# Two tiles share each gate/up block, memory folding in per-head units, casts and x spills in small pieces

## Chip, cores, metric

The kernel runs on the 8 cores of one Trainium2 chip, the same program on each with its own half of a sequence. The metric is the device time of the slowest core in microseconds (us). Most executions agree within 0.3%. Some fall into a slower state, in which one die (cores 0 to 3 or 4 to 7) or both show a lower granted TensorE clock. Fast runs are compared with fast runs.

## The reference, cut

```python
for l in range(2):                                        # D=1024, D_FF=2816, float32 inputs
    x = x + 0.5 * swiglu(rms_norm(x), gate1[l], up1[l], down1[l])      # FFN 1
    h = rms_norm(x); q, k, v, u = split(h @ w_in[l])
    x = x + concat(norm(window_attention(q, k, v)), norm(pooling(u))) @ w_out[l]
    x = x + memory_cross_attention(rms_norm(x), rms_norm(mem), wq[l], wkv[l], wo[l])
    x = x + 0.5 * swiglu(rms_norm(x), gate2[l], up2[l], down2[l])      # FFN 2
return rms_norm(x)
```

## The kernel before

A core computes 4224 tokens in 9 tiles of 512 or 384. Its weights come as float32 blocks, 128 x 2048. A cast DMA on the GpSimd (POOL) queue makes bf16 of a block at first use; a block that is used again is written back as bf16 and from then on loaded from there on the SyncE (SP) queue. Blocks land in a ring of 6 buffers for the FFN (`sb_fr`) and of 4 for the rest (`sb_mr`).

The program is a list of "visits". Each has FFN 2 of tile t-1, the mixer of tile t and FFN 1 of tile t+1, interleaved, so that TensorE has FFN matmuls while the mixer's other engines work. I number them: visit 1 is FFN 1 of tile 0 alone, visit 2 has the mixer of tile 0 and FFN 1 of tile 1, visit 3 is the first with all three, and so on to 20. The second layer's mixer begins in visit 11.

All waits are made by one helper from records of what was last written and read; an engine executes its waits and its DMA issues in program order:

```python
def dma(self, qn, out_ap, in_ap, reads=(), writes=(), box=None):
    e = self.E[qn]
    self._wait(e, self._deps(reads, writes))     # for the last writer AND readers of all of `writes`
    ...
    e.h.dma_start(out=out_ap, in_=in_ap).then_inc(box.sem, 16)
```

Which blocks are cast, and which of them are written back (`s` is the number of the block, `occ` counts its earlier uses):

```python
KEEP = 17
def route(kind, a, s, occ):          # -> (cast from float32, write back as bf16)
    if kind == "wf" and a == 0:      # FFN 1 of the first layer
        if occ == 0: return True, s >= KEEP
        if occ == 1 and s < KEEP: return True, True
    elif kind == "wf" and a == 1 and occ == 0: return True, True
    ...
```

The second layer's weights are cast in the background, three blocks (1.5 MB) to a DMA; x is stored and loaded as one DMA of up to 2 MB per tile:

```python
def load_x(v):   ... P.dma("pool", xs[s][:, :, :T], src[:, :, c0:c0 + T], ...)
def store_x(ti, l): ... P.dma("pool", x1_d[:, :, c0:c0 + T], xs[s][:, :, :T], ...)
```

Memory folding makes, once per layer, the products of memory's keys and values with the query and output weights. It runs whole in the visit of tile 0's mixer. Its last part stores each output block in four pieces:

```python
for s in range(4):
    P.dma("pool", dv[:, s, :, h, :], sv[:, s, :, :], reads=(ob_,), writes=(wabuf[l][4 + h],), box=...)
```

The order inside a visit, around x and the rope tables (sines and cosines of the positions, for the rotation of q and k; `ropes[0]` loads the positions, the rest computes, mostly on VectorE):

```python
fs += merge(gu1[6:], final_steps(*F2) + [load_x(v + 2)] + segw + seg3 + ropes)   # cut
```

The softmax here doesn't subtract the row's maximum and nothing guards it: scores larger than these inputs give would overflow.

## Time and profile before

5436.08 us, median of 6 runs (5428.8 to 5441.26).

Three lines of the page's second part, in 40 slices of the 5429.4 us span: busy tenths of TensorE, its granted clock, and the busy share of the DMA engines.

```profile
PE   7766999999999989999999899999999999999988
PEclk9887999999999999999999999999999999999999
DMA  9973975857666776887755545444454545455545
```

TensorE is at its limit nearly everywhere except in the first four slices. The table of stretches of the same core, cut at visits 1, 2, 3, then 4 to 10, visit 11, and so on; busy time (and instructions) of each engine, granted clock, DMA share, GB/s:

```profile
core 3: us, PE busy (x) PEld busy (x) DVE busy (x) ACT busy (x) POOL busy (x), PEclk, DMA share, GB/s
0.00:167.00 167.00, 126.89 (x537) 52.85 (x537) 44.19 (x75) 32.65 (x51) 41.11 (x61) 0.98 0.96 190
167.00:544.20 377.20, 241.31 (x1110) 109.75 (x1110) 118.14 (x193) 111.48 (x181) 78.34 (x104) 0.81 0.69 158
544.20:863.10 318.90, 302.26 (x1419) 134.62 (x1418) 141.31 (x217) 89.60 (x147) 60.52 (x71) 0.99 0.80 208
863.10:2841.70 1978.60, 1915.93 (x9868) 946.18 (x9866) 887.70 (x1479) 579.05 (x1006) 308.92 (x322) 0.99 0.70 195
2841.70:3174.40 332.70, 305.29 (x1639) 157.54 (x1637) 130.96 (x212) 114.58 (x203) 63.94 (x69) 0.97 0.54 185
```

And what TensorE waited for, in all, in the list of waits (total us, times, longest):

```profile
PE ps L343 <- POOL sb_ach L448: 70.0, 32, 15.2
PE ps L343 <- DMA sb_mr<-wx: 39.9, 7, 14.2
PE ps L343 <- DMA sb_fr<-wfb: 39.4, 11, 9.5
PE ps L343 <- DMA sb_fr<-wf: 33.2, 24, 4.3
```

The reader should see that visit 2 (167 to 544 us) has a clock of 0.81 and 241 us of matmul in 377. `sb_mr<-wx` are the folding's casts, `sb_fr<-wfb` loads of ready bf16 weights, `sb_ach` the sum of squares in front of a norm.

A measure used from here on: the **loss** of a visit is its duration less the columns of its matmuls divided by 2.4 GHz. All matmuls together carry 4962 us of columns. A full visit of 512-tiles in the second layer took 304.3 us for 297.6 of columns, a loss of 6.7. Of this about 3.6 us is the rate: in the trace a group of eight 512-column matmuls follows the last after 1.727 us, 215.9 ns each, where 512/2.4 is 213.3, and 2.6/213.3 of 297.6 is 3.6. The Trainium skill, "TensorE: Matmul & The Clock Gate", Part 1, gives N / 2.4 GHz + about 2.5 ns for warm matmuls, and the trace agrees.

### The profile page before, as it was taken

Reading aid. Unit: us, or ns where it says so; the run is one execution under the profiler, and the core shown is the slowest. Engines: PE = TensorE matmul, PEld = TensorE weight load, DVE = VectorE, ACT = ScalarE, POOL = GpSimd, SP = SyncE. Lnnn points to the kernel's source line nnn. Section 1 sums busy time; section 2 is a strip of 40 time slices with the busy share of each in tenths; the row PEclk is TensorE's granted clock in tenths of the full one; section 3 lists DMA queues with packets and bytes.
Section 4 is the critical chain, followed back from the end, with each engine's and each line's share of the span. In section 5 each row is a group of like instructions: output and inputs, shape, how many; then the busy total and the mean of one; then the engine's idle time right before and its main releaser. Section 6 shows DMA issues by size and latency. Waiting matters only on the chain.

```text
span 5429.4 us, 79466 instructions; the slowest of 8 cores (5401.3 to 5429.4 us)
## 1 busy us (share of the span) xinstructions
PE 5073.9 (93%) x25858; PEld 2481.2 (46%) x25858; DVE 2335.9 (43%) x3804; ACT 1645.2 (30%) x2816; POOL 980.7 (18%) x1065
## 2 busy tenths in 40 slices
PE   7766999999999989999999899999999999999988
PEld 3232444444444444555545444444444445455545
DVE  2422534445453534453536144453535344445353
ACT  1232222223232222233323323232323223233342
POOL 2212212111111112011111121211111121212211
PEclk9887999999999999999999999999999999999999
DMA  9973975857666776887755545444454545455545
GB/s 184 216 167 104 227 217 155 207 168 194 168 191 189 186 206 179 233 217 226 216 167 200 176 165 171 149 169 152 136 182 144 175 150 187 163 197 190 197 156 166
DMA packets 258878, 983.42 MB, mean 181 GB/s; under 512 B 29648, under 2 KB 30048, under 8 KB 256768
## 3 DMA queue, kind: packets, MB, share of 16 engines
q1 hardware_dynamic: 216000, 784.00, 44.1%
q0 software_dynamic: 41904, 193.29, 17.6%
q8 instruction: 222, 3.64, 0.3%
q14 instruction: 176, 1.44, 0.1%
q10 hardware_dynamic: 576, 1.05, 0.1%
HBM read 996.44 MB, written 134.35 MB: 208 GB/s over the span
## 4 chain that ended last, share of the span: by engine, by line
PE 79%; DMA 12%; DVE 3%; ACT 3%; issue 2%; POOL 1%; DVEq 0%; ACTq 0%; POOLq 0%; SPq 0%
PE ps L343 79%; DMA sb_fr<-wfb 3%; DMA sb_fr<-wf 3%; DMA wfb<-sb_fr 2%; DMA wab<-sb_mr 2%; ACT sb_tmp L149 1%; POOL sb_ach L448 1%; DMA sb_mr<-wx 1%; ACT sb_sqf L149 1%; POOL sb_acc L448 0%; ACT L146 0%; DVE sb_pT L986 0%; DMA sb_x<-xT 0%; DMA sb_ao<-memT 0%; DMA sb_mr<-wm 0%
## 5 line engine op out<-in xcount | busy, mean ns | idle before, releaser
L343 PE MATMUL ps<-sb_hF,sb_fr 128*128 128x512 bf16 (+1 forms) x12672 | 2629.3, 364 | 68.2 <-DMA sb_fr<-wfb 36.9
L343 PEld LDWEIGHTS ps<-sb_hF,sb_fr 128*128 128x128 bf16 x12672 | 1243.9, 98 | 1353.6 <-issue 122.1
L343 PE MATMUL ps<-sb_act,sb_fr 128*128 128x512 bf16 (+1 forms) x6336 | 1322.9, 363 | 22.2 <-DMA sb_fr<-wf 17.3
L528 DVE TENSOR_TENSOR sb_act<-ps,sb_sg 128x512 bf16<-128x512 f32 (+1 forms) x792 | 508.0, 645 | 1379.9 <-PE ps L343 1092.5
L448 POOL TENSOR_TENSOR sb_acc<-sb_acc,sb_sqf 128x512 f32<-128x512 f32 (+2 forms) x528 | 633.1, 1201 | 2176.4 <-ACT sb_sqf L149 2172.5
L343 PEld LDWEIGHTS ps<-sb_act,sb_fr 128*128 128x128 bf16 x6336 | 615.6, 98 | 679.1 <-issue 63.4
L343 PE MATMUL ps<-sb_hM,sb_mr 128*128 128x512 bf16 (+1 forms) x3600 | 786.1, 364 | 48.0 <-DVE sb_hM L476 27.5
L149 ACT ACTIVATE sb_sg<-ps 128x512 f32<-128x512 f32 (+1 forms) x792 | 438.6, 558 | 1153.6 <-PE ps L343 988.1
L149 ACT ACTIVATE sb_sqf<-sb_x 128x512 f32<-128x512 f32 (+1 forms) x560 | 330.5, 592 | 1019.6 <-DVE sb_x L863 438.8
L343 PEld LDWEIGHTS ps<-sb_hM,sb_mr 128*128 128x128 bf16 x3600 | 353.8, 98 | 419.5 <-issue 66.0
L149 ACT ACTIVATE sb_pT<-ps 128x512 bf16<-128x512 f32 (+2 forms) x436 | 233.8, 567 | 359.0 <-PE ps L343 357.3
L564 DVE SCALAR_TENSOR_TENSOR sb_x<-ps,sb_x 128x512 f32<-128x512 f32 (+1 forms) x288 | 184.7, 642 | 283.6 <-PE ps L343 282.7
L343 PE MATMUL ps<-sb_pT,sb_mr 128*128 128x512 bf16 (+2 forms) x1280 | 259.3, 354 | 33.6 <-DVE sb_pT L986 23.1
L476 DVE SCALAR_TENSOR_TENSOR sb_hF<-sb_x,sb_vecs,sb_rst 128x512 bf16<-128x512 f32 (+1 forms) x288 | 227.3, 841 | 11.6 <-ACT sb_rst L149 11.6
L986 DVE TENSOR_TENSOR sb_pT<-sb_pT,sb_tmp 128x512 bf16<-128x512 bf16 (+1 forms) x144 | 101.2, 744 | 302.2 <-ACT sb_tmp L149 278.4
L343 PEld LDWEIGHTS ps<-sb_pT,sb_mr 128*128 128x128 bf16 x1280 | 124.7, 98 | 161.2 <-issue 47.9
L476 DVE SCALAR_TENSOR_TENSOR sb_hM<-sb_x,sb_vecs,sb_rst 128x512 bf16<-128x512 f32 (+1 forms) x288 | 185.6, 707 | 3.8 <-ACT sb_rst L149 3.8
L149 ACT ACTIVATE sb_tmp<-sb_tmp 128x512 f32<-128x512 f32 (+1 forms) x204 | 125.8, 617 | 161.2 <-DVE sb_tmp L783 147.8
L1014 DVE TENSOR_TENSOR sb_x<-ps,sb_x 128x512 f32<-128x512 f32 (+1 forms) x144 | 93.2, 647 | 184.2 <-PE ps L343 184.2
L448 POOL TENSOR_TENSOR sb_ach<-sb_acc,sb_sqf 128x512 bf16<-128x512 f32 (+2 forms) x100 | 116.6, 1166 | 303.6 <-PE ps L343 156.7
L863 DVE TENSOR_TENSOR sb_x<-ps,sb_x 128x512 f32<-128x512 f32 (+1 forms) x144 | 92.7, 644 | 138.1 <-PE ps L343 138.1
L652 DVE TENSOR_TENSOR sb_tmp<-ps,sb_sin 64x512 f32<-64x512 f32 (+1 forms) x180 | 116.0, 644 | 48.0 <-PE ps L343 36.2
(97 smaller groups left out, 2211.7 us busy)
## 6 DMA issues: line engine op xcount, KB each, us to landing
sb_fr<-wfb SPq DMA_DIRECT2D x1105, 512.0 KB, 4.3
sb_mr<-wmb SPq DMA_DIRECT2D x153, 512.0 KB, 4.4
sb_mr<-wab SPq DMA_DIRECT2D x144, 512.0 KB, 4.3
sb_fr<-wf POOLq DMA_DIRECT2D x83, 512.0 KB, 15.0
wfb<-sb_fr SPq DMA_DIRECT2D x66, 512.0 KB, 12.3
wfb<-wf POOLq DMA_DIRECT2D x22, 1536.0 KB, 17.4
x<-sb_x POOLq DMA_DIRECT2D x6, 2048.0 KB, 14.5
sb_x<-x POOLq DMA_DIRECT2D x6, 2048.0 KB, 11.2
```

Source lines behind the costliest of these rows:

```text
L149: return self.op("act", lambda h: h.activation(out=out, in_=in_, func=func, scale=scale, **kw), reads, writes)
L343: P.op("pe", lambda h: h.matmul(out_ap, lt, rh, start=st, stop=sp_, skip_group_check=True), reads=list(rb), writes=(ob_,), signal=(i == n ...
L448: P.op("pool", lambda h: h.tensor_tensor(out=o[:, :T], in0=acc[a][:, :T], in1=sqf[s][:, :T], op=ALU.add), (accb[a], sqfb[s]), (ob_,))
L476: P.op("dve", lambda h: h.scalar_tensor_tensor(out=out_ap, in0=in_ap, scalar=vcol(col), in1=r[0], op0=ALU.mult, op1=ALU.mult), (in_b, r[1] ...
L528: P.op("dve", lambda h: h.tensor_tensor(out=actF[:, hc, :T], in0=d[1][0][:, :T], in1=sg[si][:, :T], op=ALU.mult), (d[1][1], sgb[si]), (act ...
L564: P.op("dve", lambda h: h.scalar_tensor_tensor(out=x_, in0=pp[:, :T], scalar=0.5, in1=x_, op0=ALU.mult, op1=ALU.add), (ppb, xb_), (xb_,))
L652: P.op("dve", lambda h: h.tensor_tensor(out=t1[lo:lo + 64, :T], in0=pp[hi:hi + 64, :T], in1=sinS[pr][lo:lo + 64, :T], op=ALU.mult), (ppb, ...
L863: P.op("dve", lambda h: h.tensor_tensor(out=x_, in0=pp[:, :T], in1=x_, op=ALU.add), (ppb, xb_), (xb_,))
L986: P.op("dve", lambda h: h.tensor_tensor(out=pT[:, pi_, :T], in0=pT[:, pi_, :T], in1=tmp[i][:, :T], op=ALU.mult), (pTb[pi_], tmpb[i]), (pTb ...
L1014: P.op("dve", lambda h: h.tensor_tensor(out=x_, in0=pp[:, :T], in1=x_, op=ALU.add), (ppb, xb_), (xb_,))
```

## The change

Its intent: make the start cheaper and smooth the bursts.

1. The first two tiles (the second is now a 384 tile) both use a gate/up block when it arrives, in visit 1. Tile 1's activations are laid over the x buffer of tile 2.
2. The folding is divided into a preparation and four units, one per head. The first layer's go between the shared gate/up blocks of visit 1, the second layer's one each into visits 6 to 9.
3. Background casts are single blocks (512 KB), x moves in four pieces.
4. Rope tables have another order, and the norms' sum matmuls come half a down group later.

The diff, cut to its core:

```diff
+    sizes.insert(1, sizes.pop())                      # tile 1 is a 384 tile
-        def convert(kind, a, s0, s1):                  # three blocks
+        def convert(kind, a, s):                       # one block
         def load_x(v):
-            P.dma("pool", xs[s][:, :, :T], src[:, :, c0:c0 + T], reads=rd, writes=tuple(xbs[s]), box=xbox[s])
+            def piece(j):
+                cs = slice(j * CPP, (j + 1) * CPP)
+                ex = tuple(a2b) if v == 2 else ()      # tile 1's activations lie over this buffer
+                P.dma("pool", xs[s][:, cs, :T], src[:, cs, c0:c0 + T], reads=rd, writes=tuple(xbs[s][cs]) + ex, box=xbox[s][j])
+            return [(lambda j=j: piece(j), 0.1) for j in range(NPC)]
@@ visits
-                seg3 = memkv_steps(M[1]) if M[0] == 0 else []
+            seg3 = unit_at.get(v, [])
+            if v == -1:                                # visit 1
+                ...
+                for hc in range(3, HCH):
+                    fl += g0[3 * hc:3 * hc + 3] + g1[3 * hc:3 * hc + 3]
+                kv0 = memkv_prep(0)
+                for h in range(4):
+                    kv0 += memkv_unit(0, h)
+                run(sprinkle(merge(fl, kv0), ...))
+                run(raw(f_dn(0, 0, 1, ("mix", 0, 0))))
-                fs += merge(gu1[6:], final_steps(*F2) + [(lambda v=v: load_x(v + 2), 0.1)] + segw + seg3 + ropes)
+                fs += merge(gu1[6:], pre_at.get(v, []) + final_steps(*F2) + segw + load_x(v + 2) + ropes + seg3)
@@ tail_steps
-            out = raw(dn[:1]) + xs_[:1] + raw(dn[1:3]) + ...
+            out += raw(dn[:2]) + xs_[:1] + raw(dn[2:4]) + ...
     [cut: rope order, act_second, first_norm for two tiles, y in pairs, first-visit loads]
```

Not in the diff: KEEP stays 17.

## The prediction

> **What bounds the kernel now.** TensorE: 93% busy (the page's busy table), 79% of the chain that ended last. Its matmuls carry 4962 us of columns at 2.4 GHz, so of the 5429 us span 467 us are not columns. I cut the trace of the slowest core into 20 visits (gate/up and down of one tile beside the mixer of another) and subtracted each visit's columns:
> - first visit (first FFN of tile 0): 167 us for 115 of columns; 28 us pass before the first gate matmul, and the down part runs at 4.9 us per cast block against 3.45 of matmul;
> - second visit (FFN of tile 1, mixer of tile 0, memory folding): 377 for 211. The table of stretches gives TensorE 66%, 74%, 43% in 200-500 us at a granted clock of 0.78, 0.86, 0.69. The list of waits names the folding's casts (39.9), a late norm of memory (15.2), hM (24.8), the first mixer weight (17.6);
> - third visit: 22 lost, its FFN 2 cast at 4.8 us per block;
> - 1778-2842 us: 69 lost, 33 of it waits for FFN weights, 15 to 38 us in flight instead of 4.3 while a 2 MB x spill, a 2 MB x load and 1.5-2 MB casts overlap;
> - second layer's folding visit (2842-3174): 37, the chain goes through wab stores;
> - the rest is near its floor: 6.7 per visit, of which 216 instead of 213 ns per matmul is 3.6.
>
> **What the change does.**
> 1. Tiles 0 and 1 use the same gate/up blocks. The second visit loses tile 1's 22 gate/up casts and their 75 us of matmul; tile 1 becomes a 384 tile, so 56 us move to visit one. 17 casts with write-back move to visit three, which then casts 50 blocks.
> 2. First layer's folding (27 us of columns) becomes filler beside gate/up, at 7 us of matmul per block, so its casts have time.
> 3. Second layer's folding is spread over four steady visits.
> 4. Casts of 512 KB, x in four pieces: bursts fit the six-block ring.
> 5. Down halves go ahead of the stat matmuls, which wait 1.8 us twice per visit.
>
> **Estimates from those durations.** Visit one: 28 start + 8 waiting for tile 1's norm + 165 (131 gate/up, 27 folding, clock slightly reduced) + 45 down = 246. Visit two: tile 0's mixer with 28 us of filler, so a chain: projections and rope 38, attention 33, output projection 17, cross attention 45, norms 14, part of the filler: 155. The Trainium skill, "TensorE: Matmul & The Clock Gate", Part 1, says an idle window halves the clock; the trace agrees (0.69 in 400-500 us), so visit two stays slow. Together 401 against 544: -143. Visit three +8. Spill region -34. Second folding -27, +6 in the four visits. Stat waits -25. End -4. Sum -219: 5436 to about 5220 us (-4%), nearly all on the critical path, since TensorE's idle time is what goes.
>
> **Right or wrong in the profile.** Visit one near 246 us, TensorE over 85% from 50 us on; visit two near 155, clock under 0.9, no waits for folding casts; the spill region's loss under 40; no dip at 3000-3130 us; waits for the stat sum from 70 to under 35 us.
>
> **What would make it wrong.** Folding casts queueing behind FFN casts on one issuing queue; visit two's bare chain longer than 155; 50 casts in visit three exceeding the DMA (+20); small pieces contending as much as large ones.

## The result

5366.41 us, median of 10 runs (5362.21 to 5374.76), against 5430.53 us for the kernel before in the same rounds (20 runs). Ratio 0.9879, 95% interval 0.9871 to 0.9888. A ratio is the mean of one kernel's fast runs over the mean of the other's fast runs of the same rounds, so it isn't quite the ratio of the medians. It is faster by 1.2% (the interval excludes 1); I had forecast about 5220 us, 4% less.

The page's three lines after, of the 5373.2 us span:

```profile
PE   7678899999999999999999999999999999999998
PEclk9889999999999999999999999999999999999999
DMA  7768977666576666777655545554444445454655
```

The low stretch is shorter but has not gone. Stretches cut at the same visits (after visit 1 ends at 300.5, visit 2 at 448.1, visit 3 at 797.2, visits 4 to 10 at 2854.9, visit 11 at 3102.5):

```profile
core 1: us, PE busy (x) PEld busy (x) DVE busy (x) ACT busy (x) POOL busy (x), PEclk, DMA share, GB/s
0.00:300.50 300.50, 221.38 (x1122) 112.36 (x1123) 66.04 (x128) 70.97 (x132) 59.19 (x98) 0.93 0.79 154
300.50:448.10 147.60, 111.13 (x533) 51.06 (x530) 83.30 (x139) 51.53 (x87) 39.89 (x43) 0.91 0.61 164
448.10:797.20 349.10, 297.18 (x1399) 134.81 (x1400) 126.11 (x216) 79.16 (x139) 69.55 (x96) 0.94 0.88 215
797.20:2854.90 2057.70, 1992.90 (x10113) 970.21 (x10111) 911.62 (x1494) 621.01 (x1073) 394.19 (x459) 0.99 0.67 195
2854.90:3102.50 247.60, 242.42 (x1414) 134.75 (x1412) 117.68 (x203) 79.78 (x143) 45.66 (x47) 1.00 0.59 193
```

And the waits that answer to those shown of before:

```profile
PE ps L351 <- DMA sb_fr<-wf: 52.0, 24, 11.6
PE ps L351 <- DVE sb_act L566: 42.6, 9, 7.6
PE ps L351 <- POOL sb_ach L458: 35.0, 23, 5.1
PE ps L351 <- DMA sb_mr<-wx: 33.4, 6, 10.1
```

Further down the same list:

```profile
PE ps L351 <- DMA sb_fr<-wfb: 2.4, 1, 2.4
```

Much came as intended: waits for ready weights fell from 39.4 to 2.4, for the sum of squares from 70.0 to 35.0. But the folding's casts are still waited for, the FFN's casts more than before, and `sb_act` is new.

Loss by visit, the median of the six cores whose traces have every matmul:

| visits | before | after |
|---|---|---|
| 1 | 51.9 | 95.5 |
| 2 | 163.0 | 47.8 |
| 3 | 22.0 | 69.7 |
| 4 to 10 (sum) | 81.4 | 89.0 |
| 11 | 38.7 | 7.9 |
| 12 to the end (sum) | 97.8 | 85.0 |

Visits 2 and 11 gave 146 us together. Visits 1 and 3 took 91 back, and visits 4 to 10 gained nothing. Three places of the trace suggest why; the experiments test each.

**Visit 1.** The GpSimd queue in order of time (start, duration, count, idle before it and what ended that):

```profile
119.03 0.69 POOL L160 DMA_DIRECT2D wab<-sb_mr  x1 [2.01 <-ACT sb_sg L150]
128.10 0.70 POOL L160 DMA_DIRECT2D wab<-sb_mr  x1 [8.39 <-DMA wab<-sb_mr]
130.90 0.67 POOL L160 DMA_DIRECT2D wab<-sb_mr  x1 [2.10 <-DMA wab<-sb_mr]
133.56 0.67 POOL L160 DMA_DIRECT2D wab<-sb_mr  x1 [1.99 <-DMA wab<-sb_mr]
134.15 0.65 POOL L160 DMA_DIRECT2D sb_mr<-wx  x1
```

The four stores of a folded block wait for one another to land, because they name one record. The next cast of folding weights stands behind them: 15 us pass between the first store and that cast. In all the queue waited 51.7 us for such landings in visit 1.

**Visit 3.** The DMA share was 1.0 from about 480 to 720 us. It casts 50 blocks where it cast 33 before, as the 17 blocks below KEEP get their second cast here, and are written back here.

**Visits 4 to 9.** The same queue, then VectorE, in visit 4:

```profile
969.55 2.96 POOL L160 DMA_DIRECT2D sb_x<-xT  x4
972.50 0.57 POOL L160 DMA_DIRECT2D sb_tmp<-posr  x1
973.06 1.04 POOL L160 DMA_DIRECT2D wxb<-wx  x2
```

```profile
986.74 0.43 DVE L636 CAST sb_sin<-sb_tmp 128x512 f32<-128x512 int32 x1 [17.32 <-DMA sb_tmp<-posr]
```

The load of positions (256 KB) is now issued right behind the four pieces of x (2 MB). It lands 14 us later, and VectorE, whose next instruction needs it, does nothing for 17.3 us. Products of gate and up wait behind it, PSUM (the buffer that TensorE writes to) isn't freed, and TensorE waits for `sb_act`. In the kernel before, x was loaded earlier in the visit and the positions landed a median of 6.9 us after issue, against 13.7 now. VectorE waited for them there too, but 6.5 to 10.5 us at a time in visits 4 to 9 and not 17 to 18, and TensorE's waits for `sb_act` were 2.5 us in all.

### The profile page after: what moved, and what is told of

It is laid out like the page before. It is cut to its first block, busy times and chain, and to the rows that moved or that the text cites. A ratio compares the mean times of both kernels' runs of the same rounds, so it can differ in the third digit from the quotient of the medians.

```text
span 5373.2 us, 79736 instructions; the slowest of 8 cores (5336.6 to 5373.2 us)
## 1 busy us (share of the span) xinstructions
PE 5078.7 (95%) x25865; PEld 2485.2 (46%) x25865; DVE 2321.3 (43%) x3808; ACT 1620.3 (30%) x2800; POOL 1038.1 (19%) x1163
## 4 chain that ended last, share of the span: by engine, by line
PE 80%; DMA 10%; DVE 3%; issue 2%; ACT 2%; POOL 1%; DVEq 0%; ACTq 0%; POOLq 0%; SPq 0%
PE ps L351 80%; DMA sb_fr<-wf 3%; DMA sb_tmp<-posr 2%; DMA wab<-sb_mr 2%; DMA wfb<-sb_fr 2%; ACT sb_tmp L150 1%; DVE sb_hF L486 1%; POOL sb_ach L458 1%; DMA sb_mr<-wx 1%; DVE sb_hM L486 0%; DVE sb_pT L1032 0%; DMA sb_x<-xT 0%; ACT sb_sqf L150 0%; ACT sb_rst L150 0%; DVE sb_x L603 0%
## 5 line engine op out<-in xcount | busy, mean ns | idle before, releaser
L351 PE MATMUL ps<-sb_hF,sb_fr 128*128 128x512 bf16 (+1 forms) x12328 | 2580.8, 366 | 86.8 <-DVE sb_act L566 37.2
L351 PEld LDWEIGHTS ps<-sb_hF,sb_fr 128*128 128x128 bf16 x12328 | 1210.9, 99 | 1352.5 <-issue 148.6
L351 PE MATMUL ps<-sb_act,sb_fr 128*128 128x512 bf16 (+1 forms) x6160 | 1292.6, 364 | 30.5 <-DMA sb_fr<-wf 22.8
L566 DVE TENSOR_TENSOR sb_act<-ps,sb_sg 128x512 bf16<-128x512 f32 (+1 forms) x770 | 495.0, 647 | 1253.8 <-PE ps L351 954.0
L351 PEld LDWEIGHTS ps<-sb_act,sb_fr 128*128 128x128 bf16 x6160 | 598.4, 98 | 675.6 <-issue 69.8
L1032 DVE TENSOR_TENSOR sb_pT<-sb_pT,sb_tmp 128x512 bf16<-128x512 bf16 (+1 forms) x144 | 87.1, 646 | 319.7 <-ACT sb_tmp L150 276.2
L150 ACT ACTIVATE sb_rst<-ps,sb_vecs 128x512 f32<-128x512 f32 (+2 forms) x119 | 77.1, 648 | 196.6 <-PE ps L351 196.4
```

The source lines that it names most:

```text
L150: return self.op("act", lambda h: h.activation(out=out, in_=in_, func=func, scale=scale, **kw), reads, writes)
L351: P.op("pe", lambda h: h.matmul(out_ap, lt, rh, start=st, stop=sp_, skip_group_check=True), reads=list(rb), writes=(ob_,), signal=(i == n ...
L566: P.op("dve", lambda h: h.tensor_tensor(out=a_, in0=d[1][0][:, :T], in1=sg[si][:, :T], op=ALU.mult), (d[1][1], sgb[si]), (ab_,))
L1032: P.op("dve", lambda h: h.tensor_tensor(out=pT[:, pi_, :T], in0=pT[:, pi_, :T], in1=tmp[i][:, :T], op=ALU.mult), (pTb[pi_], tmpb[i]), (pTb ...
```

## Experiments

All outputs are right. An "undisturbed die" is one at the clock of fast runs in an execution whose other die was slow; its slowest core is quoted. For the kernel before such dies gave 5418 to 5447 us. Losses of visits are medians over cores with complete records; where the profile fell in the slow state (KEEP 0, both kinds of store, large pieces, and one die of KEEP 9) over those of the undisturbed die alone.

### Positions first

```diff
-  fs += merge(gu1[6:], pre_at.get(v, []) + final_steps(*F2) + segw + load_x(v + 2) + ropes + seg3)
+  fs += merge(gu1[6:], pre_at.get(v, []) + final_steps(*F2) + ropes[:1] + segw + load_x(v + 2) + ropes[1:] + seg3)
```

> The changed kernel with one edit: the 256 KB load of positions is issued before the output projection and before the four x loads, instead of right behind them. My theory: in visits three to nine the positions land 12 to 18 us after issue because they queue behind 2 MB of x, VectorE waits 17 to 21 us for them in order, and TensorE then runs out of PSUM (waits for sb_act 33 us from 797 to 2600 us, and 11 us once in visit three). Then VectorE's waits for positions fall from 155 to under 60 us, TensorE's waits for sb_act from 43 to under 10, and the time by 30 to 50 us, to 5315 to 5335. Rival: the loss of visits three to nine is DMA traffic of the many small casts; then the positions' wait goes, but weight waits take its place and the time falls by less than 10 us.

Five undisturbed dies took 5327 to 5334 us, as expected; it was run again:

> The first experiment again, since no run of it was in the fast state. On the undisturbed dies it took 5327 to 5334 us where the kernel before took 5427 to 5447, so about 0.981 of it: 5325 to 5340 us expected in fast runs, 30 to 40 below the changed kernel's 5366. If the positions' wait was not the cause, 5355 to 5370.

One fast run, 5329.6 us (kernel before in fast runs of the same sitting: 5425.8 to 5433.3), and six dies at full clock with 5326 to 5334. That is 36 us below 5366. Who waited for the positions' tile, changed kernel first, then this one:

```profile
  DVE sb_sin L636: 155.5, 9
```

```profile
  DVE sb_sin L636: 26.6, 2
```

TensorE's wait for `sb_act` fell with it:

```profile
PE ps L351 <- DVE sb_act L566: 8.2, 3, 4.6
```

The loss of visits 4 to 9 went from 84.5 to 53.2 us. So the order of two loads is shown to be the cause of the loss there, and the rival (small casts as traffic) is refuted for this part. Visit 3 had such a wait too (11 us of TensorE's), and yet lost 67.9 instead of 69.7: there it wasn't the limit.

### Shared blocks all written back at once

```diff
-KEEP = 17
+KEEP = 0
```

> The changed kernel with KEEP 0 instead of 17: all 22 shared gate/up blocks are written back as bf16 in the first visit, so visit three casts 33 blocks and not 50 and loads 17 as bf16. Theory: visit three loses 70 us because its DMA engines are full (busy share 1.0 from 480 to 720 us); then it loses 35 to 45, the first visit gains under 10 because its DMA has room (share 0.7), and the time falls by 20 to 35 us. Rival: visit three is slow from latency of the cast chain (15 us cast, 12 us write-back, six buffers), not from the number of casts: its first 33 casts go as slowly as before, and the time falls by less than 10. Second rival: the DMA is full in the first visit too, and that visit gets 20 us or more longer.

Undisturbed dies: 5340 to 5347 us, about 23 below the changed kernel. Visit 3 lost 31.2 instead of 69.7; visit 1 lost 105.0 instead of 95.5. The stretch 480 to 720 us of core 1, changed kernel first, then this one:

```profile
480.00:720.00 240.00, 195.87 (x926) 87.61 (x925) 85.84 (x145) 50.29 (x89) 48.40 (x72) 0.94 1.02 240
```

```profile
480.00:720.00 240.00, 216.67 (x1038) 98.72 (x1039) 93.45 (x152) 56.52 (x97) 40.37 (x57) 0.98 0.89 228
```

The DMA share fell from 1.02 to 0.89 and TensorE worked 21 us more. Visit 3 was bound by the number of casts with their write-backs, as expected; latency of the chain alone is refuted. Visit 1, whose DMA share had been 0.79 and not 0.7, paid about 10 for the 17 added write-backs, not the 20 of the second rival.

### Stores that don't wait for one another

The four pieces of a folded block get records of their own (`wab4[l][h][s]`), and the readers wait for all 16.

```diff
-  P.dma("pool", dv[:, s, :, h, :], sv[:, s, :, :], reads=(ob_,), writes=(wabuf[l][4 + h],), box=abbox[d["o"]])
+  P.dma("pool", dv[:, s, :, h, :], sv[:, s, :, :], reads=(ob_,), writes=(wab4[l][h][s],), box=abbox[d["o"]])
-  rd = tuple(buf[a][4:]) if kind == "wab" and s >= 4 else (buf[a][s],)
+  rd = tuple(b_ for r_ in wab4[a] for b_ in r_) if kind == "wab" and s >= 4 else (buf[a][s],)
```

> The changed kernel, with the four 128 KB stores of each folded output block no longer waiting for one another (each piece has its own record; the readers wait for all 16). Still on the GpSimd queue. If the chain of landings in this queue holds back the casts of the next block: the waits for landed wab stores on that queue in the first visit fall from 52 to under 25 us, TensorE's waits for wx casts from 33 to about 20, and the time falls by 10 to 20 us. If the first visit is bound by DMA throughput instead, it stays within 5 us.

The gain was larger than I expected: undisturbed dies took 5325 to 5335 us, some 36 below the changed kernel. (One run took 5412 us, with both dies at a lower clock, 0.96 to 0.98.) Visit 1 took 260.7 us instead of 294.9 at a clock of 0.98 instead of 0.93, and TensorE's wait for folding casts fell from 33.4 to 6.2:

```profile
PE ps L352 <- DMA sb_mr<-wx: 6.2, 3, 3.2
```

The queue at the same place now:

```profile
119.92 2.82 POOL L160 DMA_DIRECT2D wab<-sb_mr  x4 [2.98 <-ACT sb_sg L150]
122.20 1.10 POOL L160 DMA_DIRECT2D sb_mr<-wx  x1
```

The cast now comes 2.3 us after the first store and not 15. DMA throughput is refuted as visit 1's main limit, since the same bytes moved in 34 us less; the share rose from 0.79 to 0.89.

### The same, issued by ScalarE

```diff
-  P.dma("pool", wab_d[l, h], o[:, :], ...)      # and the four pieces
+  P.dma("act", wab_d[l, h], o[:, :], ...)
```

> As the one before, and all folded stores are issued by ScalarE's own queue, so that the casts behind them in the GpSimd queue wait neither for ScalarE's copies nor for landings. If the order of one queue is what makes the first visit 300 us and not the predicted 246: the first visit falls by 30 to 45 us, TensorE's waits for wx casts under 10 us, and the time falls by 30 to 45. If DMA throughput is the limit: within 10 us of the changed kernel.

A miss. Undisturbed dies 5330 to 5352 us; visit 1 took 278.9, longer than with the stores on GpSimd. The wait for casts did fall (3.6 us at most), but a new one took its place:

```profile
PE ps L352 <- ACT sb_mr L150: 28.0, 3, 14.8
```

ScalarE's copies waited up to 21 us at a time for the landing of earlier stores from the same ring buffer. Why those landed late, up to 33 us after issue, I didn't settle. The order of one queue matters, but moving the stores to the engine that feeds TensorE is not the cure.

### Large pieces again

Casts in threes and x whole, with the positions first.

```diff
-  def convert(kind, a, s): ...                 # 512 KB
+  def convert(kind, a, s0, s1): ...            # 1.5 MB
-  return [(lambda j=j: piece(j), 0.1) for j in range(NPC)]
+  return [(lambda j=j: piece(j), 0.1) for j in range(NPX)]     # NPX = 1
```

> The positions loaded first, and the background casts again in threes (1.5 MB) and x stored and loaded whole (2 MB), as in the kernel before; all else as changed. If the small pieces are what took away the waits for prefetched FFN weights (39 us before, 2.4 after), those waits come back to 25 to 45 us in 800 to 2850 us and the time is 20 to 40 us above the run with the positions first alone. If those waits went for another reason (the 384 tile moved away from its neighbours, folding spread), it stays within 10 us of it.

Two fast runs, 5345.1 and 5353.8 us, ratio to before 0.985 (0.9826 to 0.9873). That is 16 to 24 us above the run with the positions first, less than I expected at its lower end. Waits for ready weights rose to 18.5 us (8.2 with small pieces), not to the 25 to 45 expected: large pieces brought back only some 10 us of the 37 that the whole change had removed. What removed the rest, the moved 384 tile or the spread folding, was not separated. Visits 4 to 9 lost 67.6 instead of 53.2. But visit 3 lost 58.2 instead of 67.9, which nobody had expected. So I separated the two:

### x whole, casts small

> The positions first, x whole (2 MB) and the casts small: which of the two kinds of small piece matters. Positions first alone: third visit lost 68, visits four to nine 53. Both large: 58 and 68. If whole x makes the waits of visits four to nine (store, then load of the same buffer behind it in the queue), then 58 and about 66, and about 5340 us; if the casts of 1.5 MB made them, 58 and about 53, and about 5320 us.

Fast runs 5323.3 to 5324.9 us, ratio 0.9791 (0.976 to 0.9823). Visit 3 lost 58.9, visits 4 to 9 59.6. By fast runs of two sittings, small casts are therefore worth about 20 to 30 us. The losses of visits 4 to 9 show only 8 of that (67.6 against 59.6), and those of visit 3 nothing, so the size is uncertain. The four pieces of x are worth nothing: about 6 us gained in visits 4 to 9, 9 lost in visit 3.

### x pieces that don't wait for one another

Why do the pieces cost in visit 3? In the changed kernel's GpSimd queue at its start:

```profile
444.87 0.75 POOL L160 DMA_DIRECT2D sb_x<-xT  x1
450.86 0.73 POOL L160 DMA_DIRECT2D sb_x<-xT  x1 [5.24 <-DMA sb_x<-xT]
455.27 0.72 POOL L160 DMA_DIRECT2D sb_x<-xT  x1 [3.68 <-DMA sb_x<-xT]
461.63 0.72 POOL L160 DMA_DIRECT2D sb_x<-xT  x1 [5.64 <-DMA sb_x<-xT]
462.35 2.71 POOL L160 DMA_DIRECT2D sb_fr<-wf  x5
```

It is the same chain once more: each piece names all of tile 1's overlaid activations as written, so each waits for the last, and five casts stand behind them for 17 us.

```diff
-  ex = tuple(a2b) if v == 2 else ()
+  ex = tuple(a2b) if v == 2 and j == 0 else ()
```

This was put on top of the three edits together (next section).

> The three together, and the four x pieces of the third tile no longer wait for one another's landing (all four named the same overlaid buffers as written; now only the first does). In the run with whole x the third visit lost 58 us and not 68, and in the trace the pieces block the casts of the third visit for 15 us. If that chain is the reason: the third visit loses about 20 us, 8 to 12 less, and the time is 5265 to 5275. If whole x was better for fewer transfers, nothing changes: 5278 to 5285.

Visit 3 lost 25.0 instead of 34.6. Two of its runs took 5270.2 and 5271.1 us; two more took 5280.6 and 5301.8 at a slightly lower clock on one die or both, so the ratio, 0.9712 (0.9678 to 0.9746), doesn't tell it from the three alone. Dies at full clock do: 5264 to 5269 us against 5273 to 5279. The queue at the start of visit 3 now:

```profile
419.45 2.92 POOL L160 DMA_DIRECT2D sb_x<-xT  x4
422.36 1.14 POOL L160 DMA_DIRECT2D sb_fr<-wf  x2
```

### The three together

Positions first, KEEP 0, folding stores unchained on GpSimd.

> Positions first, all shared blocks written back at once, stores of folded blocks unchained on the GpSimd queue. The three should add, as they act in different visits: first visit about 265 us (295 less 34, plus some of the 10 that writing back cost), third about 300, visits three to nine 35 less in all. 5366 less 36, 30 and 34 is 5266; 5255 to 5285 us expected, 0.970 of the kernel before. If write-backs and stores contend in the first visit, 5285 to 5310.

Fast runs 5280.3 and 5280.9 us, ratio to before 0.9723 (0.97 to 0.9746). Once more:

> The three together once more, as its profile fell in the slow state: 5275 to 5285 us in fast runs; first visit about 265 to 275 us, third about 310 with 30 lost, visits four to nine 50 lost in all. If the first visit loses more than 80, write-backs and stores contend there.

Fast runs 5279.0, 5280.0 and 5280.5, ratio 0.971 (0.9686 to 0.9734). Visit 1 lost 76.6, visit 3 34.6, visits 4 to 9 47.9. The single gains sum to 36 + 23 + 36 = 95; together they gave 86. About 6 of the missing 9 are in visit 1: it loses 76.6 where the unchained stores alone left 61.4, so write-backs cost it about 15 once the chain was gone, and not 10. The page of this kernel with the x pieces unchained, 5268.2 us:

```profile
PE   7878999999999999999999999999999999999998
PEclk9999999999999999999999999999999999999999
```

### Half the blocks written back

The last kernel with KEEP 9.

> The last kernel with KEEP 9: 13 shared blocks written back in the first visit, 9 cast again in the third. Writing back 17 more blocks cost the first visit about 10 to 14 us and gave the third 38. If the third visit's later part has room for 9 casts (its gate/up of tile 2 has the output projection beside it), the first visit loses about 68 instead of 75, the third 25 to 30, and the time is 5263 to 5270. If each cast in the third visit costs its share of 38 us, the third loses 45 and the time is 5278 to 5286.

Its one fully undisturbed run took 5280.2 us (another, 5353.6 us, had one die at a clock of 0.97). Visit 1 lost 70.8 instead of 75.1, visit 3 44.4 instead of 25.0: each cast put back into visit 3 costs about 2 us there, and saves half a us in visit 1. KEEP 0 is better.

### The second layer's folding in one visit

Positions first, and all four units in visit 9.

```diff
-  unit_at.setdefault(min(4 + h, ntl - 1), []).extend(memkv_unit(l, h))
+  unit_at.setdefault(7, []).extend(memkv_unit(l, h))
   [cut: the normed memory is loaded once, in visit 9]
```

> The positions loaded first, and the second layer's folding done in one visit (the ninth, beside gate/up of one tile) instead of over four. If spreading over four is what removed the 37 us of the folding visit: that visit loses 20 to 35 us and the four visits get back 2 each; the time rises by 10 to 30 us over the run with the positions first alone. If it is enough that the folding stands beside gate/up a visit earlier: within 8 us of it.

Fast runs 5367.4 and 5369.0 us, 38 above the spread version's one fast run, more than expected. Visits 6 to 9 lost 65.9 in all instead of 36.7, visit 9 alone 49.9. With the stores of a block still chained, spreading is what removed the loss of visit 11 before; to stand beside gate/up is not enough. The chain was at work in visit 9 too: there the GpSimd queue waited 44.6 us for landings of folded stores, and TensorE 15.4 us for ScalarE's copies into their buffers. Whether one visit would do once the stores are unchained was not tested.

## Why the prediction was wrong

The direction and most mechanisms were right; what failed were the sum itself and the durations of visit one, visit three and the spill region (visits 4 to 10). Of my checks in the profile, "no waits for folding casts" in visit two and "no dip at 3000-3130 us" came true, visit two ended 8 us under its 155 and its clock was about 0.9, and the waits for the stat sum were 35.0. Visit one was 49 us longer, with TensorE busy 79% from 50 us on and not 85, and the spill region I had listed (visits 7 to 10) lost about 50 and not under 40. Of the 155 us between my sum (219 less than the kernel before, 5430.5 in these rounds) and 5366, by loss:

- **An error of my own sum, 27 us.** "Together 401 against 544: -143" compared durations. With tile 1 at 384 tokens, visits 1 and 2 carry 298.2 us of columns, before 325.3. These 27 us weren't removed; they moved to later visits.
- **Visit one, 49 us.** Predicted 246, measured 295. Of the terms, the start held (28 predicted, 28.9 measured). From the first gate matmul to the first down matmul I had 8 + 165 = 173 and the trace has 210; for the down part I had 45 and it has 55. With the stores unchained these are 183 and 49. I had named "folding casts queueing behind FFN casts on one issuing queue" as a risk; it was the stores of folded blocks, waiting for one another, that held the casts back. Unchaining them alone gave 34 of the 49. The clue stood in the profile before: I read there that the second folding's chain "goes through wab stores", and still took the first folding for hidden work.
- **Visit two, 8 us the other way.** Predicted 155, measured 147 at a clock of 0.90. The bare mixer chain was costed well in sum; I didn't compare its pieces.
- **Visit three, 40 us.** Predicted 8 more than the 22 lost, measured 69.7. My step "17 casts with write-back move to visit three" was right, its size was not: I took 4.8 us per block from FFN 2's part and fitted them into FFN 1's time, and gave it 8 us, although I had listed "50 casts in visit three exceeding the DMA (+20)" as a risk: the DMA engines were full for 240 us. That x's load comes there too I had left out. Writing back at once took 38 of it away, unchaining x's pieces another 10.
- **Visits four to ten, 36 us.** Predicted -28 (-34 for the spills, +6 for folding), measured +8. The waits I aimed at did go (for ready weights 39.4 to 2.4), though small pieces are shown as the reason for only some 10 us of it; and the gain was given back by a wait I didn't see, for positions loaded behind x. Putting them first gave 31.
- **Second folding, 4 us better than thought.** Predicted -27, measured -31.
- **Stat waits and end, 16 us.** Predicted -29 over all visits, measured -13 in visits 12 to the end; a part that falls into earlier visits is counted there. The waits did halve, 70.0 to 35.0, as I wrote; but a steady visit's loss fell only from 6.7 to 4.8 us.

These sum to 27 + 49 - 8 + 40 + 36 - 4 + 16 = 156. With the four repairs the kernel takes about 5270, still 50 above my forecast; 27 of that is the wrong sum. What remains of visit 1 (75 lost) I didn't take apart further; the 29 us before the first gate matmul are part of it.

## What to carry to other kernels

When one transfer is divided into pieces, give every piece its own dependency record, and look in the trace at what stands behind the pieces in the same issuing queue: a wait for a landing there delays every later transfer, however unrelated. A small load that an in-order engine needs next should be issued before a large one, not after it. When work is moved between stretches, compare the time lost beyond the matmul columns, not the durations, or moved work counts as saved; and ask of the stretch that receives it whether its DMA engines still have room.

## What the Trainium skill lacked or had wrong

- "DMA: Bandwidth & Descriptors", section "Rules for kernel authors", asks for at least 1 MiB per DMA for the highest bandwidth. It lacks what that does to other streams: with background casts of 512 KB instead of 1.5 MB beside prefetched weights, fast runs of two sittings took 5324 against 5345 to 5354 us (only 8 us of this are found in the losses of visits 4 to 9). For x, 2 MB whole was as good as four pieces.
- The same page, "Issuing engines are not separate DMA queues", says that issuing from several engines saves only the sequencer's time. It gives no figure for a queue that waits for a landing between its issues: here four stores of 128 KB held the next cast back by 15 us, and removing those waits took 34 us off one visit.
- The same page, "Two DMAs through the same engine are not ordered", says that within one queue of one DMA engine descriptors start in order. The trace agrees (in visit 4 the four pieces of x landed at 977.6 to 985.3 us and the positions, issued behind them, at 986.6), and the page gives no cost: 256 KB issued behind 2 MB on the GpSimd queue (192 behind 1.5 for a 384 tile) landed a median of 13.7 us after issue, and 8.5 us when issued ahead of it; these are medians of all nine loads, and of the seven in visits 3 to 9 they are 12.9 and 7.3.
- "TensorE: Matmul & The Clock Gate", Part 1, expects 13/16 of the clock once three cores of a die run dense matmuls, for as long as the load lasts. In fast runs all eight cores ran dense matmuls at a granted clock of 0.99 to 1.00 in most visits. Only slow runs fit the page: one showed 0.817 to 0.820 on all cores and 6159 to 6188 us.
